# Narrow products kept together in a list schedule, attention bias strips read from DRAM, and a shorter inverse square root

## The chip, the cores and the metric

The kernel runs on one core of one Trainium2 chip. The metric is the device time of one execution in microseconds; lower is better. The whole program is one launch: two transformer-like blocks of two layers each, on 256 tokens of width 1024, batch one.

## The reference, cut to what matters

The first block has two layers of attention and feed-forward. Its attention adds a bias to the logits that depends on the distance of query and key alone (`rel_bias` looked up by `rel_bucket(q - k)`, for 12 heads), masks keys behind the query, and takes a softmax. Queries, keys and the attention's output are normalised by their root mean square. The second block mixes a short convolution, attention over latent and context tokens and a gated linear attention in each of two layers, modulated by vectors that come from `silu(c) @ w_ada`.

```python
logits = einsum(q, k) * scale + bias_tab[rel_bucket(qpos - kpos)]
logits = where(qpos >= kpos, logits, -inf); p = softmax(logits)
rms_norm(x, g) = x * rsqrt(mean(x * x) + 1e-6) * g
mod = silu(c) @ w_ada + b_ada        # and the same for c_ctx
```

Everything is in float32. The weights, about 270 MB, are read from DRAM once.

## The kernel before

**Tiling.** Activations lie transposed, 128 channels to a tile and 256 or 512 tokens along the free axis. Each weight arrives as a `raw` tile of 128 by 1024 (512 KB) by the sync queue (SP), is split into a rounded high part `wH` by ScalarE (ACT) and a remainder `wL` by VectorE (DVE), and each product is three passes of TensorE (PE): high by high, high by low, low by high (`mm3`). Layer 0 of the first block runs four head pairs one after another (`attention1`): two with `diff_pair`, two with `moba_pair`; then the output projection and the feed-forward (`ffn`).

**The order of the work.** The program records every operation (`record`) and then sets the order itself (`order`): a list schedule over five engines, with a cost for each operation, a latency, a priority (the place in the program) and limits on tiles. On each engine the operation of lowest priority number that is ready goes next. The engines then run their lists in that order, each waiting on semaphores where its data isn't there. Since every operation is issued from `emit` (L442), every row of the profile has that line, and groups are told apart by tiles. `nc.after` gives an operation one more predecessor in the schedule only; on the chip it makes no wait.

**Narrow products.** Column sums (`gsum`, tiles `xsq`, `qsq`, `osq`, `gsq`, `ksq` by a constant of 32 columns into a tile `ms`) and the modulation vectors (`mod_part`, tile `wada` by `cs`) are products whose stationary side has 32 columns. Four of them write the four quarters of the partitions of one PSUM tile. Each float32 product is two instructions, so a group of four is eight. The schedule's `cost` gives a whole product's time to the first of a group and 27 ns to each of the others.

**Bias strips.** `bias_strips` makes a row for every head (tile `brow`, 12 partitions by 384, in SBUF) of bias by distance, with the mask added. `bias_strip` spreads a head's row over 128 partitions, each shifted by one element, by a DMA of the ACT queue from the one partition that holds the row: 12 DMAs of 128 KB, two for each of 6 tiles `strip`. They are recorded once for each of layer 0's four pairs: one tile for each of the first two, two for each of the last two. `attn_scores` adds them to the scores on DVE (`sb<-x,s,strip`). Layer 1 uses the same strips again.

**Roots.** `rsqrt` works on small tiles (`s`, 1 to 16 columns) on DVE: a shift and a subtraction of the bits, and three Newton steps of three instructions; 12 instructions with the first addition, 13 with a scale. It is called 42 times, the last two in `out_last`, where the result is made.

Of the kernel before, what the change touches and what calls it, by code (L numbers as in the profile page):

```python
# [26 lines left out]
EPS = 1e-6  # L27
NEG = -1.0e30
MAGIC = 0x5F3759DF
AHEAD = {"ps": 12, "T": 16, "Q": 14}  # L30
ROLES = {"mm": 4, "x4": 4, "ms": 3, "raw": 4, "H": 7, "L": 7, "ada": 4}
NT, NQ = 24, 24
# [41 lines left out]

class Op:
    __slots__ = ("i", "eng", "fn", "args", "kw", "cost", "lat", "prio", "deps", "succ", "nd", "ready", "start", "end",
                 "new", "uses", "dma", "table", "alloc")


class _Proxy:  # L80
# [51 lines left out]
class Rec:  # L132


    def __init__(self, tc):
        self.tc, self.nc = tc, tc.nc
        nc = tc.nc
        self.vector, self.scalar, self.tensor = _Proxy(self, "DVE", nc.vector), _Proxy(self, "ACT", nc.scalar), _Proxy(self, "PE", nc.tensor)
        self.gpsimd, self.sync = _Proxy(self, "POOL", nc.gpsimd), _Proxy(self, "SP", nc.sync)
        self.ops, self.tiles, self.caps, self.psum, self.acc, self.role = [], {}, {}, set(), {}, {}  # L140
        self.seen, self.old = {}, set()
        self.offset = 0.0
        self.ahead, self.rolecap = {}, {}
        self.after = None

    def pool(self, ctx, name, bufs, **k):
        p = ctx.enter_context(self.tc.tile_pool(name=name, bufs=bufs, **k))
# [15 lines left out]
    def box(self, ap):  # L163
        pat = ap.ap
        ps, pn = pat[0]
        ps = ps or 1
        p0, f0 = divmod(ap.offset, ps) if pn > 1 or ps > 1 else (0, ap.offset)
        f1 = f0 + 1
        for s, c in pat[1:]:
            f1 += s * (c - 1)  # L170
        return p0, p0 + pn, f0, f1

    def cost(self, eng, method, out, args, kw):
# [38 lines left out]
    def record(self, eng, method, fn, args, kw):  # L212
        o = Op()
        o.i, o.eng, o.fn, o.args, o.kw = len(self.ops), eng, fn, args, kw
        o.prio = o.i + self.offset
        out = kw["out"] if "out" in kw else args[0]
        outs = [out] + ([kw["accum_out"]] if kw.get("accum_out") is not None else [])
        ins = [a for a in (args if "out" in kw else args[1:]) if isinstance(a, bass.AP)]
        ins += [a for k, a in kw.items() if isinstance(a, bass.AP) and k not in ("out", "accum_out")]
        o.lat = LAT[eng]  # L220
        o.table = TABLES.get(args[2]) if eng == "ACT" and method == "activation" else None
        o.dma = method == "dma_start"
        if method == "dma_start":
            o.lat = 0
        src_args = (out,) + tuple(args if "out" in kw else args[1:])
        o.cost = self.cost(eng, method, out, src_args, kw)
        deps, o.alloc = set(), set()
        o.uses = set()
        o.new = []
        if method == "dma_start":  # L230
            nb = self.free(out) * out.ap[0][1] * 4
            o.lat = nb
        for ap, w in [(a, False) for a in ins] + [(a, True) for a in outs]:
            tn = ap.tensor.name
            if tn not in self.tiles:
                continue
            if tn in self.old:
                pass
            elif tn not in self.seen:
                self.seen[tn] = o.i  # L240
                o.new.append(tn)
                o.uses.add(tn)
            else:
                o.uses.add(tn)
                o.alloc.add(self.seen[tn])
            b = self.box(ap)
            lst = self.acc.setdefault(tn, [])
            bank = tn in self.psum
            c = b
            if bank and eng == "PE" and w and (kw.get("start") or method == "transpose"):  # L250
                c = (b[0], b[1], 0, 1 << 30)
            keep = []
            for (pb, pi, pw, pe) in lst:
                if w or pw:
                    hit = pb[0] < c[1] and c[0] < pb[1] and pb[2] < c[3] and c[2] < pb[3]
                    if hit or (bank and pe != eng):
                        deps.add(pi)
                    if w and b[0] <= pb[0] and pb[1] <= b[1] and b[2] <= pb[2] and pb[3] <= b[3] and pi != o.i:
                        continue
                keep.append((pb, pi, pw, pe))  # L260
            keep.append((b, o.i, w, eng))
            self.acc[tn] = keep
        if self.after is not None:
            deps.add(self.after)
        deps.discard(o.i)
        o.alloc -= deps
        o.alloc.discard(o.i)
        o.deps = deps
        self.ops.append(o)

    def order(self):
# [73 lines left out]

        done = 0
        total = len(ops)
        while done < total:
            best = None
            for e in engs:  # L350
                t0 = t_eng[e]
                while future[e] and future[e][0][0] <= t0:
                    r, p, i = heapq.heappop(future[e])
                    heapq.heappush(avail[e], (p, i))
                if avail[e]:
                    s = t0
                elif future[e]:
# [5 lines left out]
            if best is None:  # L363
                raise RuntimeError("deadlock: " + str({k: [(ops[i].fn.__name__, ops[i].args[:1]) for i in v][:2] for k, v in parked.items() if v})[:2000])
            s, e = best
            t_eng[e] = max(t_eng[e], s)
            while future[e] and future[e][0][0] <= s:
                r, p, i = heapq.heappop(future[e])
                heapq.heappush(avail[e], (p, i))
            p, i = heapq.heappop(avail[e])  # L370
            o = ops[i]
            d = PATIENCE.get(e, 0)
            if d and o.cost > d:
# [41 lines left out]
            for j in o.succ:  # L415
# [7 lines left out]
                q.nd -= 1  # L423
                if q.nd == 0:
                    push(q)
            for tn in o.uses:
                left[tn] -= 1
                fin[tn] = max(fin.get(tn, 0.0), vis)
# [19 lines left out]
class Emit:  # L448
# [148 lines left out]

    def rsqrt(self, src, n, scale=None, shape=None, guard=None, more=None):
        nc = self.nc
        tiles = [self.small(n) for _ in range(5)] + [self.small(n, I32)]  # L600
        v, y, t, u, r, h = tiles
        sh = (lambda q: q) if shape is None else (lambda q: q.rearrange(shape[0], **shape[1]))
        bits = lambda q, dt: q.bitcast(dt)
        if more is not None:
            nc.vector.scalar_tensor_tensor(v, src, EPS, more, ALU.add, ALU.add)
        elif guard is None:
            nc.vector.tensor_scalar(sh(v), src, EPS, None, ALU.add)
        else:
            nc.vector.tensor_tensor(out=sh(v), in0=src, in1=guard, op=ALU.add)
        nc.vector.tensor_scalar(h, bits(tiles[0], I32), 1, None, ALU.logical_shift_right)  # L610
        nc.vector.tensor_scalar(bits(tiles[1], I32), h, -1, MAGIC, ALU.mult, ALU.add)
        for i in range(3):
            nc.vector.tensor_tensor(out=t, in0=y, in1=y, op=ALU.mult)
            nc.vector.scalar_tensor_tensor(u, t, -0.5, v, ALU.mult, ALU.mult)
            nc.vector.scalar_tensor_tensor(y, u, 1.5, y, ALU.add, ALU.mult)
        if scale is not None:
            nc.vector.tensor_scalar(r, y, scale, None, ALU.mult)
            return tiles[4]
        return tiles[1]

    def gsum(self, ps, sqs, ones, start=True, stop=True):

        nc = self.nc
        nc.after = max(nc.last(sq) for sq in sqs)
        for g, sq in enumerate(sqs):
            nc.tensor.matmul(ps[32 * g:32 * g + 32, :self.free(sq)], self.c(ones), sq, start=start, stop=stop)
        nc.after = None

    def gcols(self, ps, ng, n):

# [57 lines left out]
    def mod_part(self, l, part, after):  # L688
# [4 lines left out]
        for kk in range(0, KT, 2):  # L693
# [5 lines left out]
            if kk % 4:  # L699
                nc.after = nc.last(raw)  # L700
                for g in range(4):
                    nc.tensor.matmul(ps[32 * g:32 * g + 32, :], self.cs[:, kk - 2 + g, :], ws[g], start=kk < 4, stop=kk >= 4)
                nc.after = None
                ws = []
        res = self.t2("adar")
        nc.scalar.activation(res, ps, AF.Copy)
# [48 lines left out]
    def bias_strips(self):  # L755
# [7 lines left out]
        nc.tensor.matmul(ps[:12, :384], rb, oh, start=True, stop=True)  # L763
        nc.vector.tensor_tensor(out=row, in0=ps[:12, :384], in1=mr, op=ALU.add)
        self.strip = [None] * 6
        self.brow = row

    def bias_strip(self, i, after):

        nc = self.nc  # L770
        st = self.t2("strip")
        nc.after = after
        for a in range(2):
            src = self.brow[2 * i + a:2 * i + a + 1, 0:T]
            win = bass.AP(tensor=src.tensor, offset=src.offset + P - 1, ap=[list(src.ap[0]), [-1, P], [1, T]])
            nc.scalar.dma_start(st[:, a * T:(a + 1) * T], win)
        nc.after = None
        self.strip[i] = st.rearrange("p (a b) -> p a b", a=2)

    def lam(self, l, init):  # L780
        nc = self.nc
# [33 lines left out]
    def attn_scores(self, pr, a, qg, kn, rq, rcol, head):  # L815
# [10 lines left out]
        for m in range(2):  # L826
# [5 lines left out]
            for t in range(2):  # L832
                nk = P * (t + 1)
                sl = slice(t * P, t * P + nk)
                nc.vector.scalar_tensor_tensor(sb[:, sl], ps[:, t * T:t * T + nk], rq[:, rcol(m, t):rcol(m, t) + 1],
                                               st[:, T - nk:T], ALU.mult, ALU.add)
                nc.vector.tensor_reduce(mx[:, t:t + 1], sb[:, sl], AX.X, ALU.max, negate=True)
                nc.scalar.activation(sb[:, sl], sb[:, sl], AF.Exp, bias=mx[:, t:t + 1], accum_out=den[:, t:t + 1])
            rc = self.small(2)
# [977 lines left out]
def constants():  # L1817
# [30 lines left out]
    for lv in range(7):  # L1848
# [1 line left out]
        seg = i // (2 * m)  # L1850
        half = (i // m) % 2
        masks[:, lv, :] = (seg[:, None] == seg[None, :]) & (half[:, None] != half[None, :])
    return {"ck": ck, "oneh": oneh.astype(np.float32), "maskr": np.ascontiguousarray(maskr.astype(np.float32)),
            "masks": masks.reshape(P, 7 * P).astype(np.float32)}


# [23 lines left out]
```

## Time and profile before

| | |
|---|---|
| three timed runs | median 2057.44 us (2056.23 to 2058.48) |
| profiled execution | 2054.4 us, its span 2052.6 us |
| PE busy | 2027.0 us (99%), 14158 instructions |
| DVE busy | 1464.4 us (71%) |
| ACT busy | 1167.6 us (57%) |
| read from DRAM | 282.51 MB, 140 GB/s over the span |

Busy time counts instructions of the engine itself; time in which an engine's sequencer waits or issues a DMA isn't counted. In the views, a row of a timeline gives the start in us, the length in us, the engine (with a q behind it: the engine's sequencer), the operation with its output and inputs, shapes and count, and in brackets the idle time ahead of it with what ended it. Neighbouring instructions of one kind are merged into one row.

### The profile page before, as it was taken

The numbers are of one execution on the slowest core, as the hardware profiler recorded it, in microseconds if no ns is written. First come the engines' busy times: TensorE is split into PE (matmuls) and PEld (weight loads), VectorE is DVE, ScalarE is ACT, GpSimd is POOL, SyncE is SP. The second block draws the span as 40 slices with busy tenths as digits, with TensorE's granted clock in tenths as the row PEclk, the third lists the DMA queues.
The fourth block names the chain that finished last, engine by engine and source line by source line (L and its number), as shares of the span: only waits on it lengthen the run. The fifth ranks groups of instructions, "written<-read, shape, count | busy, mean of one in ns | idle before, by whom it ended". The sixth has DMA issues, their size and how long they took to land.

```text
span 2052.6 us, 35592 instructions
## 1 busy us (share of the span) xinstructions
PE 2027.0 (99%) x14158; PEld 1847.7 (90%) x14158; DVE 1464.4 (71%) x2846; ACT 1167.6 (57%) x2055; POOL 8.7 (0%) x20
## 2 busy tenths in 40 slices
PE   9989999999999999999999999999999999999998
PEld 7879999989999989988888888888888999999997
DVE  7778986888866699983477755563467888696663
ACT  6656656767665767762366323333357777575542
POOL 0000000000000000000000000000000000000000
PEclk9999999999999999999999999999999999999999
DMA  9765665555555121232122543342361225436551
GB/s 296 140 166 200 225 226 174 185 175 175 206 185 196 60 74 64 72 120 86 53 72 72 193 135 122 115 140 96 135 214 67 89 83 186 141 116 215 176 190 68
DMA packets 86846, 292.68 MB, mean 143 GB/s; under 512 B 9452, under 2 KB 17176, under 8 KB 86424
## 3 DMA queue, kind: packets, MB, share of 16 engines
q1 hardware_dynamic: 81544, 281.50, 39.6%
q10 hardware_dynamic: 5136, 8.91, 2.8%
q8 instruction: 111, 1.82, 0.4%
q14 instruction: 55, 0.45, 0.1%
HBM read 282.51 MB, written 4.19 MB: 140 GB/s over the span
## 4 chain that ended last, share of the span: by engine, by line
PE 97%; DMA 1%; DVE 1%; ACT 0%; issue 0%; ACTq 0%; SPq 0%; DVEq 0%
PE mm L442 78%; PE x L442 11%; PE acc L442 6%; PE ms L442 2%; DMA strip<-brow 1%; DVE s L442 0%; DMA xx<-in_xt_dram 0%; ACTq L442 0%; ACT h L442 0%; DVE wL L442 0%; DVE sb L442 0%; ACT y L442 0%; ACT wH L442 0%; ACT xg L442 0%; DVE h L442 0%
## 5 line engine op out<-in xcount | busy, mean ns | idle before, releaser
L442 DVE TENSOR_TENSOR wL<-raw,wH 128x1024 fp32r<-128x1024 f32 (+1 forms) x472 | 569.7, 1217 | 307.0 <-PE mm L442 144.6
L442 ACT ACTIVATE wH<-raw 128x1024 fp32r<-128x1024 f32 (+1 forms) x472 | 491.5, 1053 | 252.2 <-DVE wL L442 112.0
L442 PE MATMUL mm<-h2H,wH 128*128 128x256 f32 (+1 forms) x1504 | 504.2, 338 | 2.1 <-ACT h2H L442 2.1
L442 PE MATMUL mm<-h2L,wH 128*128 128x512 f32 (+2 forms) x1504 | 504.0, 337 | 0.0
L442 PE MATMUL mm<-h2H,wL 128*128 128x256 f32 (+1 forms) x1472 | 497.5, 338 | 0.0
L442 PEld LDWEIGHTS mm<-h2H,wH 128*128 128x128 f32 x1504 | 283.6, 190 | 33.2 <-issue 3.5
L442 PEld LDWEIGHTS mm<-h2L,wH 128*128 128x128 f32 (+1 forms) x1504 | 283.2, 189 | 28.7 <-issue 1.6
L442 PEld LDWEIGHTS mm<-h2H,wL 128*128 128x128 f32 x1472 | 279.3, 190 | 28.6 <-issue 1.0
L442 PE MATMUL mm<-h,wH 128*128 128x256 f32 x1216 | 219.6, 283 | 0.0
L442 PEld LDWEIGHTS mm<-h,wH 128*128 128x128 f32 x1216 | 189.6, 192 | 0.0
L442 PE MATMUL mm<-h,wL 128*128 128x256 f32 x608 | 172.0, 283 | 0.0
L442 PE MATMUL mm<-xg,wH 128*128 128x256 f32 x704 | 133.9, 289 | 1.5 <-ACT wH L442 1.5
L442 PE MATMUL acc<-hid,wH 128*128 128x256 f32 x704 | 128.2, 284 | 0.0
L442 PEld LDWEIGHTS mm<-h,wL 128*128 128x128 f32 x608 | 116.7, 192 | 0.0
L442 PEld LDWEIGHTS mm<-xg,wH 128*128 128x128 f32 x704 | 112.1, 195 | 4.0 <-ACT wH L442 1.9
L442 PE MATMUL mm<-xL,wH 128*128 128x512 f32 (+1 forms) x320 | 111.4, 348 | 0.0
L442 PE MATMUL mm<-xH,wL 128*128 128x512 f32 (+1 forms) x320 | 111.2, 348 | 0.0
L442 PE MATMUL mm<-xH,wH 128*128 128x512 f32 (+1 forms) x320 | 111.0, 348 | 0.0
L442 PEld LDWEIGHTS acc<-hid,wH 128*128 128x128 f32 x704 | 109.8, 192 | 0.8 <-issue 0.8
L442 PE MATMUL mm<-xg,wL 128*128 128x256 f32 x352 | 101.6, 290 | 0.2 <-DVE wL L442 0.2
L442 PE MATMUL acc<-hid,wL 128*128 128x256 f32 x352 | 98.4, 283 | 0.0
L442 ACT ACTIVATE gt<-mm,hb 128x512 f32<-128x512 f32 (+1 forms) x48 | 27.8, 579 | 116.1 <-PE mm L442 116.0
(295 smaller groups left out, 3850.5 us busy)
## 6 DMA issues: line engine op xcount, KB each, us to landing
raw<-in_w_dram SPq DMA_DIRECT2D x272, 512.0 KB, 3.7
raw<-in_w1up_dram SPq DMA_DIRECT2D x88, 512.0 KB, 4.1
wada<-in_wada_dram SPq DMA_DIRECT2D x48, 512.0 KB, 5.4
raw<-in_w1in_dram SPq DMA_DIRECT2D x46, 512.0 KB, 5.9
raw<-in_w1dn_dram SPq DMA_DIRECT2D x44, 512.0 KB, 4.4
raw<-in_w1out_dram SPq DMA_DIRECT2D x16, 512.0 KB, 4.5
crow<-in_crow_dram SPq DMA_DIRECT2D x6, 512.0 KB, 6.4
qh<-qh SPq DMA_DIRECT2D x16, 128.0 KB, 2.2
```

Of the source, the lines that this page charges most:

```text
L442: o.fn(*o.args, **o.kw)
```

## The change

It has three parts. Operations recorded while `join` is set are scheduled directly behind the operation recorded before them, if they are ready then; `gsum` and `mod_part` set it for the second to fourth product of a group. `brow` is now a tile in DRAM: the sync queue stores the rows there, and loads each `strip` (both heads, 256 KB) by one DMA, with 128 overlapping windows. The rows are stored in reverse and the strip is read with a step of -1 by DVE. `rsqrt` becomes nine instructions, with the scale folded in, and takes five small tiles.

```diff
@@ def order(self):
+        must = None
+        gone = set()
 ...
+            if must is not None:
+                e, i = ops[must].eng, must
+                p, s = ops[i].prio, max(t_eng[e], ops[i].ready)
+                gone.add(i)
+                must = None
+            else:
 ...
+            if o.i + 1 < total and ops[o.i + 1].join and ops[o.i + 1].nd == 0:
+                must = o.i + 1
@@ def rsqrt(self, src, n, scale=None, shape=None, guard=None, more=None):
-        nc.vector.tensor_scalar(h, bits(tiles[0], I32), 1, None, ALU.logical_shift_right)
-        nc.vector.tensor_scalar(bits(tiles[1], I32), h, -1, MAGIC, ALU.mult, ALU.add)
-        for i in range(3):
-            nc.vector.tensor_tensor(out=t, in0=y, in1=y, op=ALU.mult)
-            nc.vector.scalar_tensor_tensor(u, t, -0.5, v, ALU.mult, ALU.mult)
-            nc.vector.scalar_tensor_tensor(y, u, 1.5, y, ALU.add, ALU.mult)
-        if scale is not None:
-            nc.vector.tensor_scalar(r, y, scale, None, ALU.mult)
+        f = RQ[0] * (1.0 if scale is None else scale)
+        nc.vector.tensor_scalar(y.bitcast(I32), v.bitcast(I32), -0.5, MAGIC, ALU.mult, ALU.add)
+        nc.vector.tensor_tensor(out=t, in0=y, in1=y, op=ALU.mult)
+        nc.vector.tensor_tensor(out=w, in0=t, in1=v, op=ALU.mult)
+        nc.vector.scalar_tensor_tensor(w, w, RQ[1], w, ALU.add, ALU.mult)
+        nc.vector.scalar_tensor_tensor(y, w, RQ[2], y, ALU.add, ALU.mult)
+        nc.vector.tensor_tensor(out=t, in0=y, in1=y, op=ALU.mult)
+        nc.vector.scalar_tensor_tensor(w, t, -0.5 * f * RQ[0] ** 2, v, ALU.mult, ALU.mult)
+        nc.vector.scalar_tensor_tensor(r, w, 1.5 * f, y, ALU.add, ALU.mult)
@@ def gsum(self, ps, sqs, ones, start=True, stop=True):
         for g, sq in enumerate(sqs):
+            nc.join = g > 0
             nc.tensor.matmul(ps[32 * g:32 * g + 32, :self.free(sq)], self.c(ones), sq, start=start, stop=stop)
@@ def mod_part(self, l, part, after):
                 for g in range(4):
+                    nc.join = g > 0
@@ def bias_strips(self):
-        self.brow = row
+        self.brow = nc.dram_tile(self.tc, [12, 384], "brow")
+        nc.sync.dma_start(self.brow, row)
+        self.bstore = len(nc.ops) - 1
@@ def bias_strip(self, i, after):
-        nc.after = after
-        for a in range(2):
-            src = self.brow[2 * i + a:2 * i + a + 1, 0:T]
-            win = bass.AP(tensor=src.tensor, offset=src.offset + P - 1, ap=[list(src.ap[0]), [-1, P], [1, T]])
-            nc.scalar.dma_start(st[:, a * T:(a + 1) * T], win)
+        src = self.brow[2 * i:2 * i + 1, 0:T]
+        win = bass.AP(tensor=src.tensor, offset=src.offset + 1, ap=[[1, P], [384, 2], [1, T]])
+        nc.after = max(after, self.bstore)
+        nc.sync.dma_start(st, win)
@@ def attn_scores(self, pr, a, qg, kn, rq, rcol, head):
+                e = st[:, nk - 1:nk]
+                bias = bass.AP(tensor=e.tensor, offset=e.offset, ap=[list(e.ap[0]), [-1, nk]])
                 nc.vector.scalar_tensor_tensor(sb[:, sl], ps[:, t * T:t * T + nk], rq[:, rcol(m, t):rcol(m, t) + 1],
-                                               st[:, T - nk:T], ALU.mult, ALU.add)
+                                               bias, ALU.mult, ALU.add)
```

The left-out lines record `join` with each operation, skip entries in the schedule's lists that were taken out of turn, let the address boxes count negative steps, and reverse the constants `oneh` and `maskr` on the host.

## Rows read from the trace of the kernel before

**Rows 1.** The page's first part: busy time of each engine.

```profile
PE 2027.0 (99%) x14158; PEld 1847.7 (90%) x14158; DVE 1464.4 (71%) x2846; ACT 1167.6 (57%) x2055; POOL 8.7 (0%) x20
```

**Rows 2.** Windows: stretch, length, busy us (count) per engine, clock, DMA share, GB/s.

```profile
8.20:60.00 51.80, 51.80 (x405) 44.96 (x406) 39.97 (x111) 38.30 (x78) 2.08 (x4) 0.97 0.97 293
60.00:91.70 31.70, 31.70 (x259) 27.99 (x257) 23.16 (x78) 18.88 (x45) 1.04 (x2) 1.00 0.70 155
91.70:138.00 46.30, 36.11 (x253) 31.02 (x252) 34.76 (x89) 27.63 (x67) 0.00 (x0) 0.96 0.75 137
...
347.80:490.20 142.40, 140.53 (x1141) 126.04 (x1141) 113.52 (x311) 98.78 (x209) 3.29 (x6) 1.00 0.53 178
```

**Rows 3.** The chain that ended last, in order of time: start, us, what.

```profile
91.78 3.79 issue
...
116.33 18.58 DMA strip<-brow
```

**Rows 4.** Timeline of ACT and its queue, layer 0 of the first block.

```profile
80.29 0.53 ACTq L442 DMA_DIRECT2D strip<-brow  x1
...
84.29 5.18 ACTq L442 DMA_DIRECT2D strip<-brow  x1
89.56 2.01 ACT L442 ACTIVATE wH<-raw 128x1024 fp32r<-128x1024 f32 x2 [6.86 <-issue]
...
113.19 8.31 ACTq L442 DMA_DIRECT2D strip<-brow  x3
```

**Rows 5.** Timeline of DVE around the bias rows and the strips' uses.

```profile
30.76 0.54 DVE L442 TENSOR_TENSOR brow<-ms,maskr 12x384 f32<-12x384 f32 x1
...
39.14 0.74 DVE L442 SCALAR_TENSOR_TENSOR sb<-x,s,strip 128x128 f32<-128x128 f32 x2 [1.14 <-DMA strip<-brow]
...
97.37 0.74 DVE L442 SCALAR_TENSOR_TENSOR sb<-x,s,strip 128x128 f32<-128x128 f32 x2
```

**Rows 6.** DMA from 80 to 100 us: queue, packets, MB, share of 16 engines.

```profile
q10 hardware_dynamic: 522, 0.48, 60.4%
```

**Rows 7.** DMA issues of the whole run: count, KB each, median us to landing.

```profile
wd<-in_wd_dram SPq DMA_DIRECT2D x8, 128.0 KB, 4.1
...
crow<-in_crow_dram SPq DMA_DIRECT2D x6, 512.0 KB, 6.4
```

**Rows 8.** Tile raw from 0 to 170 us: the weights' landing times.

```profile
DMA to landing us min/median/max: 3.1/6.5/15.1
```

**Rows 9.** Timeline of PE at narrow products, broken groups and a whole one.

```profile
44.69 1.90 PE L442 MATMUL x<-wada,cs 128*32 128x512 f32 x10
...
70.14 1.04 PE L442 MATMUL x<-wada,cs 128*32 128x512 f32 x2
71.12 0.55 PE L442 MATMUL x<-ck,sb 128*128 128x128 f32 x3
71.59 1.06 PE L442 MATMUL x<-wada,cs 128*32 128x512 f32 x8
...
109.78 0.62 PE L442 MATMUL ms<-qsq,ck 128*32 128x256 f32 x2
110.33 0.86 PE L442 MATMUL x<-at,v 128*64 128x256 f32 x4
...
152.63 0.64 PE L442 MATMUL ms<-xsq,ck 128*32 128x256 f32 x8
```

**Rows 10.** Timeline of DVE in the last root, and its use.

```profile
2045.80 0.15 DVE L442 SCALAR_TENSOR_TENSOR s<-s 128x1 f32<-128x1 f32 x1
...
2048.10 1.42 DVE L442 SCALAR_TENSOR_TENSOR y<-og,s,xt 128x512 f32<-128x512 f32 x2
```

**Rows 11.** Timeline of PE in layer 1: a wait for a root.

```profile
393.56 0.65 PE L442 MATMUL ms<-ck,s 128*128 128x128 f32 x4 [1.27 <-DVE s L442]
```

**Rows 12.** Timeline of the sync queue in layer 0.

```profile
57.45 8.85 SPq L442 DMA_DIRECT2D raw<-in_w1in_dram  x3
75.35 1.18 SPq L442 DMA_DIRECT2D qh<-qh  x2
```

More of the change, by code (lines that the diff above doesn't have):

```diff
@@ L29 @@
 MAGIC = 0x5F3759DF
+RQ = (0.3755374238926038, -3.334362783627379, 4.997213710402795)
 AHEAD = {"ps": 12, "T": 16, "Q": 14}
@@ L76 @@
     __slots__ = ("i", "eng", "fn", "args", "kw", "cost", "lat", "prio", "deps", "succ", "nd", "ready", "start", "end",
-                 "new", "uses", "dma", "table", "alloc")
+                 "new", "uses", "dma", "table", "alloc", "join")
 class _Proxy:
@@ L144, in __init__ @@
         self.after = None
+        self.join = False
     def pool(self, ctx, name, bufs, **k):
@@ L169, in box @@
         for s, c in pat[1:]:
-            f1 += s * (c - 1)
+            if s < 0:
+                f0 += s * (c - 1)
+            else:
+                f1 += s * (c - 1)
         return p0, p0 + pn, f0, f1
@@ L215, in record @@
         o.prio = o.i + self.offset
+        o.join = self.join
         out = kw["out"] if "out" in kw else args[0]
@@ L351, in order @@
                 t0 = t_eng[e]
-                while future[e] and future[e][0][0] <= t0:
+                while future[e] and (future[e][0][0] <= t0 or future[e][0][2] in gone):
                     r, p, i = heapq.heappop(future[e])
                     heapq.heappush(avail[e], (p, i))
+                while avail[e] and avail[e][0][1] in gone:
+                    heapq.heappop(avail[e])
                 if avail[e]:
@@ L365, in order @@
             s, e = best
[L366 to L370, printed above, removed]
+            if must is not None:
[3 more added lines that the diff above has]
+                must = None
+            else:
+                t_eng[e] = max(t_eng[e], s)
+                while future[e] and future[e][0][0] <= s:
+                    r, p, i = heapq.heappop(future[e])
+                    if i not in gone:
+                        heapq.heappush(avail[e], (p, i))
+                p, i = heapq.heappop(avail[e])
             o = ops[i]
@@ L599, in rsqrt @@
         nc = self.nc
-        tiles = [self.small(n) for _ in range(5)] + [self.small(n, I32)]
-        v, y, t, u, r, h = tiles
+        v, y, t, w, r = tiles = [self.small(n) for _ in range(5)]
         sh = (lambda q: q) if shape is None else (lambda q: q.rearrange(shape[0], **shape[1]))
-        bits = lambda q, dt: q.bitcast(dt)
         if more is not None:
@@ L609, in rsqrt @@
             nc.vector.tensor_tensor(out=sh(v), in0=src, in1=guard, op=ALU.add)
-        nc.vector.tensor_scalar(h, bits(tiles[0], I32), 1, None, ALU.logical_shift_right)
-        nc.vector.tensor_scalar(bits(tiles[1], I32), h, -1, MAGIC, ALU.mult, ALU.add)
-        for i in range(3):
-            nc.vector.tensor_tensor(out=t, in0=y, in1=y, op=ALU.mult)
-            nc.vector.scalar_tensor_tensor(u, t, -0.5, v, ALU.mult, ALU.mult)
-            nc.vector.scalar_tensor_tensor(y, u, 1.5, y, ALU.add, ALU.mult)
-        if scale is not None:
-            nc.vector.tensor_scalar(r, y, scale, None, ALU.mult)
-            return tiles[4]
-        return tiles[1]
+        f = RQ[0] * (1.0 if scale is None else scale)
[7 more added lines that the diff above has]
+        nc.vector.scalar_tensor_tensor(r, w, 1.5 * f, y, ALU.add, ALU.mult)
+        return r
     def gsum(self, ps, sqs, ones, start=True, stop=True):
@@ L625, in gsum @@
         for g, sq in enumerate(sqs):
+            nc.join = g > 0
             nc.tensor.matmul(ps[32 * g:32 * g + 32, :self.free(sq)], self.c(ones), sq, start=start, stop=stop)
-        nc.after = None
+        nc.after, nc.join = None, False
     def gcols(self, ps, ng, n):
@@ L701, in mod_part @@
                 for g in range(4):
+                    nc.join = g > 0
                     nc.tensor.matmul(ps[32 * g:32 * g + 32, :], self.cs[:, kk - 2 + g, :], ws[g], start=kk < 4, stop=kk >= 4)
-                nc.after = None
+                nc.after, nc.join = None, False
                 ws = []
@@ L765, in bias_strips @@
         self.strip = [None] * 6
-        self.brow = row
+        self.brow = nc.dram_tile(self.tc, [12, 384], "brow")
+        nc.sync.dma_start(self.brow, row)
+        self.bstore = len(nc.ops) - 1
     def bias_strip(self, i, after):
         nc = self.nc
-        st = self.t2("strip")
-        nc.after = after
-        for a in range(2):
-            src = self.brow[2 * i + a:2 * i + a + 1, 0:T]
-            win = bass.AP(tensor=src.tensor, offset=src.offset + P - 1, ap=[list(src.ap[0]), [-1, P], [1, T]])
-            nc.scalar.dma_start(st[:, a * T:(a + 1) * T], win)
+        st = self.t2("strip").rearrange("p (a b) -> p a b", a=2)
+        src = self.brow[2 * i:2 * i + 1, 0:T]
+        win = bass.AP(tensor=src.tensor, offset=src.offset + 1, ap=[[1, P], [384, 2], [1, T]])
+        nc.after = max(after, self.bstore)
+        nc.sync.dma_start(st, win)
         nc.after = None
-        self.strip[i] = st.rearrange("p (a b) -> p a b", a=2)
+        self.strip[i] = st
     def lam(self, l, init):
@@ L1852, in constants @@
         masks[:, lv, :] = (seg[:, None] == seg[None, :]) & (half[:, None] != half[None, :])
-    return {"ck": ck, "oneh": oneh.astype(np.float32), "maskr": np.ascontiguousarray(maskr.astype(np.float32)),
+    return {"ck": ck, "oneh": np.ascontiguousarray(oneh[:, ::-1].astype(np.float32)), "maskr": np.ascontiguousarray(maskr[:, ::-1].astype(np.float32)),
             "masks": masks.reshape(P, 7 * P).astype(np.float32)}
```

## The prediction

> **What bounds the kernel now.** I read the busy times first: PE is busy for 2027.0 us of a span of 2052.6, while DVE has 71% and ACT 57% [rows 1]. So the end is PE's work plus PE's pauses, and a change can win only by taking work off PE, by closing a pause, or by shortening what follows PE's last product. Then I asked where the 25.6 us of pauses lie, by windows. From 8.2 to 91.7 us PE has none; from 91.7 to 138 us it is busy 36.11 of 46.30 us, so 10.19 us are lost in the attention of layer 0; the attention and output projection of layer 1, the same work with the strips already there, lose 142.40 - 140.53 = 1.87 us [rows 2]. The rest is the start, the tail behind the last product, and waits of under 2 us. The third view was the chain of waits: in the stretch that loses 10 us it goes through "issue" for 3.79 us at 91.78 and through one strip's DMA for 18.58 us at 116.33 [rows 3]. The timeline of ACT says what that is. Issuing one strip took ACT's queue 5.18 us, and three more 8.31 us; behind the first ones ACT sat idle 6.86 us before it could split the next weight [rows 4]. PE's pause at 91.78 follows from that. The second cause is the transfer itself: from 80 to 100 us the queue that carries the strips moved 0.48 MB and held the 16 DMA engines 60.4% of the time [rows 6], so 0.604 x 20 = 12.1 us of all engines for 0.48 MB, or 40 GB/s, where the stretch before 60 us moves 293 GB/s [rows 2].
>
> **The strips.** Removed: 12 DMAs on ACT's queue. Added: one store of 18 KB and six loads of 256 KB on the sync queue. The store and a load can't be seen in this trace. The nearest row is `wd`, 256 pieces of 512 bytes from DRAM to 128 partitions, landing after 4.1 us; `crow`, 512 KB read by all partitions from the same 4 KB of DRAM, takes 6.4 us among other traffic [rows 7]. A strip has 256 pieces of 1 KB from one small region; I take 5 us from issue to landing, with 4.1 below, and above the 18.58 us that the slowest strip takes now. Strips 2 and 3 are issued at 80.29 and first used at 97.37 [rows 4, 5]; 17 us hold even a doubled landing time. So I count the strip pauses as gone except what layer 1 also has: 10.19 - 1.87 = 8.3 us. ACT is relieved of the issue time, and DVE, PE and the weights of their waits for it, in the same stretch.
>
> Strip 0 gets a detour. Its rows are ready at 31.3 and its first use, at 39.14, already waits 1.14 us for it [rows 5]. The store goes behind the weights; at their median landing time of 6.5 us [rows 8] it lands at about 37.8, and the load behind it at 41.9 to 44.2. The first scores are then 3 to 5 us later. In this stretch PE has no pause [rows 2] and other products to run, and weights no longer queue behind two slow strips; I charge 1.0 us, between 0 and 5. The issues themselves, seven on the sync queue, cost nothing there: that queue issued nothing between 66.3 and 75.35 [rows 12] while PE was fully busy.
>
> [...]
>
> **Groups kept together.** A group of four is eight instructions and takes 0.64 us at 256 columns, a piece of two 0.62 [rows 9]: the four run beside each other, so a piece costs what the whole does. A broken group costs another 0.55 us (109.78 to the next product at 110.33). I counted four such groups, at 48.65, 109.78, 385.51 and 411.06: 2.2 us. For the modulation (512 columns) a whole group takes 1.06 us and a lone product 0.98 (70.14 to 71.12) [rows 9]; two are broken so, at 70.14 and 1543.65: 1.9 us. Three more, at 44.69, 408.97 and 438.22, show as ten instructions in 1.90 us, a group with the first product of the next behind it: 1.90 - 1.06 = 0.84 each, 2.5 us. Two groups at 79.3 lie interleaved, and about 0.1 us is lost when they are parted. Sum: 6.5 us. All lie where PE is the limit, or will be once the strips are gone, so I count all of it. Should the forced order not reach the chip, it is 0.
>
> **Roots.** The last root is on the path behind PE's last product: 12 instructions from 2045.80 to 2048.10, 0.19 us each [rows 10]. Three fewer give 0.6 us. Of the others, 42 calls in all, the one that shows as a wait of PE for a root, 1.27 us in layer 1 [rows 11], gets shorter by the same 0.6. The rest, 42 x 3 x 0.19 = some 24 us of DVE, is hidden by PE's work.
>
> **The reversed read** of the strip on DVE isn't in this trace. The 64 additions have the same elements and bytes; I take 0. If it were at half speed, each of 0.37 us (0.74 for two [rows 5]) would cost up to 0.4 more, 13 us of DVE in each layer, where DVE is free 142.40 - 113.52 = 29 us [rows 2]; a quarter to a half on the chain is 3 to 6 us a layer at worst. I see no gain in it.
>
> **Sum.** 8.3 + 6.5 + 0.6 + 0.6 - 1.0 = 15.0 us. The profiled execution took 2054.4, its span 2052.6; that makes 2039.4. The median of the timed runs is 3.0 above the profiled one, so I forecast 2057.44 - 15.0 = 2042.4.
>
> **Rivals.**
>
> *The strips were a symptom.* If the attention of layer 0 is held by its chain of small steps, the 10.19 us come back as other waits, and 2057.44 - 6.5 - 1.2 + 1.0 = 2050.7 remains. For it: all engines are busy 70 to 80% there. Against it: layer 1 does the same with 1.87 us. 10%.
>
> *Groups aren't kept together on the chip*, or their pieces ran in time that PE had to spare: 2042.4 + 6.5 = 2048.9. For it: 4 of the 9 broken groups lie ahead of or between the strips' pauses, which could have absorbed them. Against: the pauses begin with ACT's release, which the forecast moves. 10%.
>
> *The reversed read is slow* or the whole order, which is redone from the new costs, is less lucky: 2 to 8 us lost, 2044 to 2050, as 2047. Waits of 1 to 2 us are now at three places, and a new order may have more. 15%.
>
> *The sync queue is blocked: slower.* Its list is in order. A strip's load waits for a free tile, and the first for the store; all weights stand behind it, then ACT and DVE that split them, then PE. It was silent for 9 us at 66.3 and PE had no pause [rows 2, 12], so 9 us are covered. With landings of 15.1 us as the longest weights have [rows 8], each of four pairs would lose 15.1 - 9 = 6.1 us, 24 us in all: 2066. It decides against the change from 9 + 15.0/4 = 12.8 us of blocking at each pair. The long landings are themselves the strips' doing, which speaks against it. 5%.
>
> **How the numbers follow.** The forecast's own case has 60%, with 2038 to 2046 from the bounds of the detour (0 to 5 us), of what layer 1 keeps (0 to 1.87) and of the waits on roots. Taking in the rivals at 2047, 2048.9 and 2050.7 up to the edge, the range is 2036 to 2051. What a measurement of this kernel can tell from no change is 0.2%, or 4.1 us: faster is below 2053.3. All cases but the blocked queue and the tails of two others lie there: faster 0.89, same 0.06, slower 0.05.
>
> **What would show it.** Right: PE's busy time falls by about 6.5 us, to 2020; every `wada`, `qsq` and `xsq` row of PE has eight instructions or a multiple; no strip on ACT's queue, and no idle of ACT for "issue" near 89; strips land in 4 to 7 us; PE's pause between 91 and 138 falls from 10.2 to about 2 us; the last root takes 1.7 us instead of 2.3. Wrong: strips that land in over 15 us, waits of DVE for strips, gaps on PE near 40 us, additions of strips over 0.5 us, or new pauses behind the first 200 us.

## The result, and the profile after

The changed kernel takes 2034.7 us (median of 4 runs, 2033.21 to 2035.8) beside 2056.84 us for the kernel before; the ratio is 0.9891 (95% interval 0.9874 to 0.9908). The forecast was 2042.4 with a range from 2036.0. The direction was right, the gain of 22.1 us half as large again as the 15.0 us forecast, and the time 1.3 us below the range.

Its profiled execution took 2035.6 us (span 2033.8), against 2054.4 (2052.6) before: 18.8 us less. The first line of its page answers to [rows 1]: PE's busy time fell by 7.6 us, DVE's by 19.9.

```profile
PE 2019.4 (99%) x14158; PEld 1846.6 (91%) x14158; DVE 1444.5 (71%) x2712; ACT 1168.7 (57%) x2055; POOL 8.6 (0%) x20
```

Windows of the changed kernel, as in [rows 2] (stretch, length, busy us of PE, PEld, DVE, ACT, POOL, granted clock, DMA share, GB/s; the last stretch is layer 1, which now lies earlier):

```profile
8.20:60.00 51.80, 49.61 (x392) 43.41 (x394) 41.03 (x101) 40.00 (x81) 2.07 (x4) 0.97 0.90 328
60.00:91.70 31.70, 31.08 (x251) 28.28 (x252) 26.77 (x78) 21.95 (x52) 1.04 (x2) 0.95 0.45 148
91.70:138.00 46.30, 45.83 (x356) 41.48 (x355) 35.61 (x89) 30.08 (x69) 0.00 (x0) 1.00 0.39 131
...
337.50:478.00 140.50, 140.50 (x1165) 129.06 (x1162) 114.03 (x297) 101.57 (x215) 3.17 (x6) 1.00 0.53 182
```

PE now loses 0.47 us between 91.7 and 138 where it lost 10.19, and nothing in layer 1 where it lost 1.87. New are some 2.5 us of short pauses between 55 and 61 us, and a granted clock of 0.95 in the stretch from 60 on. The strips' own rows show why the long pauses are gone (instructions of the tile: min/median/max ns, first and last start; then the landing times):

```profile
L462 DVE SCALAR_TENSOR_TENSOR sb<-x,s,strip x64: 324/405/478, 47.1 to 442.5; 128x128 f32<-128x128 f32 x32, 128x256 f32<-128x256 f32 x32
L462 SPq DMA_DIRECT2D strip<-brow x6: 380/426/932, 36.3 to 105.1; - x6
...
DMA to landing us min/median/max: 5.2/5.6/7.4
```

Strips land after 5.6 us, not 11.6, no instruction waits for one, and the reversed read costs nothing: its 64 additions took 327/406/477 ns before. On PE every row of `wada`, `qsq` and `xsq` now has eight instructions, or sixteen where two groups stand side by side (timeline, as in [rows 9]). One `osq` group still runs in two pieces, at 58.65 and 59.96 us, because its second half isn't ready: it waits 0.90 us for ACT.

```profile
47.27 0.64 PE L462 MATMUL ms<-qsq,ck 128*32 128x256 f32 x8
47.72 1.90 PE L462 MATMUL x<-wada,cs 128*32 128x512 f32 x16
...
396.07 1.92 PE L462 MATMUL x<-wada,cs 128*32 128x512 f32 x16
```

PE's rows for the modulation products fell from 17.3 to 12.3 us and those for `qsq` from 12.0 to 9.4, 7.6 us together. The last root takes 1.73 us (2027.75 to 2029.48) instead of 2.30 [rows 10]:

```profile
2027.75 0.15 DVE L462 SCALAR_TENSOR_TENSOR s<-s 128x1 f32<-128x1 f32 x1
...
2029.48 1.41 DVE L462 SCALAR_TENSOR_TENSOR y<-og,s,xt 128x512 f32<-128x512 f32 x2
```

By the profile, then: 10.4 us of pauses of PE, 7.6 us of its busy time, 0.8 us of the tail. In the forecast these were 7.3 + 0.6, 6.5 and 0.6. The other 3.3 us lie between profile and timed runs: the kernel before is 2.4 us slower in its timed runs than in its profiled execution (3.0 by the three runs that the forecast had), the changed one 0.9 us faster.

### The profile page after: what moved, and what is told of

Read it like the earlier page. It is cut to its first block, busy times and chain, and to the rows that moved or that the text cites. A ratio compares the mean times of both kernels' runs of the same rounds, so it can differ in the third digit from the quotient of the medians.

```text
span 2033.8 us, 35473 instructions
## 1 busy us (share of the span) xinstructions
PE 2019.4 (99%) x14158; PEld 1846.6 (91%) x14158; DVE 1444.5 (71%) x2712; ACT 1168.7 (57%) x2055; POOL 8.6 (0%) x20
## 4 chain that ended last, share of the span: by engine, by line
PE 98%; DMA 1%; ACT 1%; DVE 0%; issue 0%; SPq 0%; DVEq 0%; ACTq 0%
PE mm L462 79%; PE x L462 11%; PE acc L462 6%; PE ms L462 2%; DMA raw<-in_w_dram 0%; DMA raw<-in_w1in_dram 0%; ACT wH L462 0%; ACT fH L462 0%; DVE s L462 0%; ACT F L462 0%; SPq L462 0%; ACT att L462 0%; ACT h L462 0%; ACT v L462 0%; DVE y L462 0%
```

## The experiments

The parts were run alone, each part was taken out of the whole, one part was varied, and one cost was measured by itself. Times are medians; the ratio is to the kernel before on the same chip. The clock is the mean granted clock of the profiled execution; busy time, and pauses up to the last product, are PE's, from the same one.

| run | time us | ratio (95%) | clock | PE busy | pauses |
|---|---|---|---|---|---|
| before (in the first set) | 2057.39 | | 0.998 | 2027.0 | 17.4 |
| e1 groups alone | 2053.11 | 0.9980 (0.9971 to 0.9989) | 0.995 | 2021.2 | 21.3 |
| e2 strips alone | 2044.51 | 0.9940 (0.9927 to 0.9954) | 0.999 | 2024.4 | 10.3 |
| e3 roots alone | 2055.35 | 0.9992 (0.9983 to 1.0001) | 0.997 | 2027.9 | 17.6 |
| e4 all | 2033.87 | 0.9884 (0.9871 to 0.9898) | 0.998 | 2016.8 | 7.9 |
| e5 all but groups | 2041.62 | 0.9919 (0.9905 to 0.9932) | 0.999 | 2023.9 | 7.1 |
| e6 all but roots | 2040.24 | 0.9913 (0.9900 to 0.9927) | 0.998 | 2019.9 | 10.1 |
| e7 strips, ACT's queue | 2045.55 | 0.9935 (0.9921 to 0.9948) | 0.998 | 2025.2 | 11.1 |
| e8 all, and pairs | 2026.10 | 0.9844 (0.9831 to 0.9858) | 0.999 | 2009.5 | 7.1 |
| e9 all but strips | 2052.82 | 0.9972 (0.9961 to 0.9984) | 0.993 | 2023.9 | 19.2 |
| e10 all, 4 short holds | 2038.23 | 0.9901 (0.9886 to 0.9916) | 0.998 | 2019.0 | 10.2 |
| e11 all, 4 long holds | 2063.99 | 1.0028 (1.0019 to 1.0038) | 0.995 | 2026.3 | 28.0 |

The kernel before was at 2058.42 in the set of e5 to e8 and at 2058.48 in that of e9 to e11, so differences across sets carry about 1 us.

**e1, groups alone.** The edit is the change's `join` and nothing else:

```diff
 ...
+            if o.i + 1 < total and ops[o.i + 1].join and ops[o.i + 1].nd == 0:
+                must = o.i + 1
 ...
+            nc.join = g > 0
 ...
```

> The kernel before with the groups of four kept together and nothing else. Theory A (the parts add up, each by its own mechanism): PE's busy time falls by the 6.5 us that I forecast, or by the 7.6 us that the changed kernel shows (2027.0 to 2019.4), no narrow row with two, six or ten instructions is left, and the time falls by as much, 6 to 8 us. Rival B (four of the nine broken groups lie ahead of or between the strips' pauses, which absorb what they give back): PE's busy time falls as much, but its pauses grow by about 2.8 us, and the time falls by 3 to 5 us.

The time fell by 4.3 us: B's size. The busy time fell by 5.8 us, and the pauses rose by 3.9, a little more than B's 2.8. Windows of e1 show the two pauses of the strips, and the clock right behind each:

```profile
87.40:90.90 3.50, 0.16 (x2) 0.07 (x1) 1.99 (x4) 3.45 (x8) 0.00 (x0) 0.97 0.79 31
90.90:94.30 3.40, 3.40 (x17) 3.40 (x18) 3.34 (x7) 2.17 (x3) 0.00 (x0) 0.53 0.80 26
...
111.50:119.40 7.90, 0.16 (x2) 0.05 (x1) 0.00 (x0) 1.43 (x3) 0.00 (x0) 0.69 0.90 124
119.40:125.00 5.60, 5.60 (x27) 5.60 (x28) 4.54 (x15) 1.79 (x2) 0.00 (x0) 0.52 0.93 132
```

PE did nothing for 3.3 and 7.7 us, and then worked for 3.4 and 5.6 us at a granted clock of 0.53 and 0.52; a product `mm<-wL,xg` of 256 columns took 0.41 us behind the second pause (at 120.27) and 0.28 ahead of it (at 111.34). That clock isn't a pause in any view: the windows count it as busy PE (3.40 of 3.40 and 5.60 of 5.60 us).

**e2, strips alone.** The change's store, loads and reversed read; groups and roots as before.

```diff
 ...
+        nc.sync.dma_start(self.brow, row)
 ...
-            nc.scalar.dma_start(st[:, a * T:(a + 1) * T], win)
 ...
+        nc.sync.dma_start(st, win)
 ...
```

> The kernel before with the strips stored to DRAM and loaded by the sync queue, and with the reversed read; groups and roots as before. Theory A: PE's pauses between 20 and 140 us fall from 10.2 to about 3 us, strips land in 5 to 7.5 us, and the time falls by 7 to 8 us. Rival C (the strips were a symptom; the shorter roots or the groups closed the pauses): the pauses stay at 6 us or more and the time falls by under 4 us.

The pauses did what theory A says, 17.4 to 10.3 in all, and no view shows the clock low between 20 and 138 us:

```profile
20.00:60.00 40.00, 39.08 (x309) 32.46 (x307) 33.40 (x96) 28.13 (x57) 1.04 (x2) 1.00 0.85 298
60.00:91.70 31.70, 30.86 (x248) 27.09 (x249) 27.04 (x87) 22.09 (x51) 1.04 (x2) 1.00 0.47 153
91.70:138.00 46.30, 45.67 (x347) 40.57 (x346) 36.07 (x93) 29.73 (x68) 0.00 (x0) 1.00 0.39 132
```

But the time fell by 12.9 us, not 7 to 8. The clock is what A left out. In the kernel before, PE worked at a granted clock of 0.64 for 4.3 us behind the strip's pause:

```profile
91.70:95.70 4.00, 0.21 (x2) 0.16 (x2) 3.37 (x6) 3.95 (x8) 0.00 (x0) 1.00 0.88 79
95.70:100.00 4.30, 4.30 (x25) 4.23 (x26) 4.27 (x12) 2.84 (x9) 0.00 (x0) 0.64 0.86 98
```

The profiles show 10.0 of the 12.9 us: 7.1 of pauses, 2.6 of busy time, and the tail. By an estimate from its clock, (1 - 0.64) x 4.3 = 1.5 of the 2.6 us stand in the second line. Not all of the rest is the strips': in the first 20 us the kernel before has a granted clock of 0.91 and 0.92, e2 of 1.00, and the changed kernel, without the strips' pauses, falls there too (0.83 from 10 to 20 us). The last 2.9 us stand in no profile: the timed runs of the kernel before, at a mean clock of 0.993 to 0.998, lie 3.0 us above its profiled one, and e2's, at 0.997 to 0.999, 0.1.

**e3, roots alone.**

```diff
 ...
-        for i in range(3):
 ...
+        nc.vector.tensor_scalar(y.bitcast(I32), v.bitcast(I32), -0.5, MAGIC, ALU.mult, ALU.add)
 ...
```

> The kernel before with the nine-instruction root alone. My forecast gave this part 1.2 us (0.6 in the tail, 0.6 in one wait). Theory A': it closes the waits of layer 1 (1.87 us) and the one before the second block's second layer (1.94 us) nearly whole, and the time falls by 3 to 4 us. Rival D: those waits went by the new order or by the other parts; here the time falls by 0.5 to 1.3 us.

The time fell by 2.0 us, between the two, and the interval of the ratio just reaches 1. The pauses of layer 1 are gone and that before the second block's second layer fell to 0.2 us, but in this order the strips' first pause was 7.3 us instead of 3.8.

**e4, the change again**, without an edit.

> The changed kernel once more on the same chip as the three parts. Theory A: its gain is the sum of the three parts within 2 us. Rival E (the order that the whole gives is lucky by itself): the sum of the parts falls short by 4 us or more. By the profile the gain is 18.8 us, by the timed runs 22.1; should the timed kernel before be 2 to 3 us above its own profiled execution here too, the difference lies in the runs of before and not in a part of the change.

The sum of the parts, 4.3 + 12.9 + 2.0 = 19.2 us, falls short of the whole, 23.5, by 4.3 us. That is E's size, but e5, e6 and e9, each with an order of its own, give a plainer reading than luck: a part pays less while another's pauses stand.

**e5, all but the groups; e6, all but the roots.** The edits take e1's and e3's lines out of the changed kernel.

> The changed kernel without the groups kept together (strips and roots as changed). The groups alone gave 4.1 us, with PE's pauses up from 17.4 to 21.3 us and two more stretches at the lower clock. Theory A2 (what the groups give back was swallowed by the strips' pauses and by the clock that falls after them): here, where those pauses are gone, the groups are worth their whole 6.5 to 7.6 us, and the time is 2040 to 2042 us. Rival B2 (a broken group costs only what was measured alone): 2037 to 2038 us.

> The changed kernel with the old root of 12 or 13 instructions. Theory A2: the shorter root closes the pauses of layer 1 (1.87 us) and before the second block's second layer (1.94 us) and 0.6 us of the tail, so without it the time is 3 to 4 us more, 2037 to 2038 us. Rival D2: as measured alone, 1 to 2 us more, 2035 to 2036 us.

With the strips' pauses gone, the groups are worth 7.7 us (6.7 with the 1.0 us between the sets taken out), and the roots 6.4 (5.3). A2 holds for the groups, and both theories were too low for the roots. e6 shows why; windows around the pause of 1.95 us before the second block's second layer:

```profile
1533.10:1535.20 2.10, 0.15 (x2) 0.09 (x1) 2.00 (x7) 1.87 (x5) 0.00 (x0) 1.00 0.00 0
1535.20:1540.00 4.80, 4.80 (x28) 4.80 (x29) 3.04 (x10) 4.80 (x13) 0.00 (x0) 0.64 0.01 3
```

and the same place in the changed kernel:

```profile
1532.00:1535.00 3.00, 2.71 (x21) 2.37 (x20) 2.84 (x9) 3.00 (x9) 0.00 (x0) 1.00 0.02 5
1535.00:1543.00 8.00, 8.00 (x70) 8.00 (x69) 4.84 (x9) 7.21 (x16) 0.00 (x0) 1.00 0.06 17
```

The old root leaves a pause of 1.95 us, and behind it the clock was 0.64 for 4.8 us: (1 - 0.64) x 4.8 = 1.7 us of PE's work, an estimate. With the new root 0.29 us of pause are left, and the clock stayed at 1.00. This isn't a matter of one order: all five profiled kernels with the old root wait 1.94 or 1.95 us there and 1.26 or 1.27 us for a root in layer 1, and none with the new root waits over 0.3 us at either place. The pauses (2.2 us), the tail (0.6) and this fall of the clock (1.7) make 4.5 of the 5.8 us between the profiled executions of e6 and e4; the rest is not explained. Such a pause isn't followed by the lower clock in every execution: the kernel before had the same 1.94 us pause, and its profile shows the clock at 1.00 behind it:

```profile
1549.20:1551.30 2.10, 0.16 (x2) 0.09 (x1) 2.00 (x7) 2.02 (x5) 0.00 (x0) 1.00 0.00 0
1551.30:1562.00 10.70, 10.70 (x90) 10.70 (x91) 7.53 (x17) 9.77 (x22) 0.00 (x0) 1.00 0.05 14
```

**e7, the strips' source against their queue.** e2 with one line back on ACT's queue:

```diff
-        nc.sync.dma_start(st, win)
+        nc.scalar.dma_start(st, win)
```

> The kernel before with strips from DRAM, but loaded by ACT's queue as before (one load for a tile, groups and roots as before). Theory S (the source decides: one partition's bytes are slow to read, which holds the DMA engines and makes the issuing queue stand): loads are issued in under 1 us each, land in 4 to 8 us, PE's pauses between 20 and 140 us are 2 to 4 us, the granted clock is 0.998 or 0.999, and the time is 2044 to 2046 us, as with the sync queue. Rival Q (ACT stands because it issues them): issues of 2 us and more and idle ACT remain, and the time is 2049 us or more.

S holds in its time (2045.55 us), its clock (0.998) and its issues (0.39 us, median). The queue makes no difference to the time that can be measured (ratios 0.9935 and 0.9940, the intervals overlap), though the loads landed after 3.8 us here and after 5.2 in e2 (medians); rows of the tile, then its landing times:

```profile
L445 ACTq DMA_DIRECT2D strip<-brow x6: 366/392/487, 40.8 to 112.9; - x6
...
DMA to landing us min/median/max: 3.3/3.8/5.6
```

ACT's issues took up to 5.2 us each before and under 0.5 us here, so it isn't ACT's issuing that makes them long. That the source in one partition makes them long is the author's estimate, from [rows 6]; e7 doesn't isolate it: with the source, the loads became one of 256 KB for two of 128 KB, and the direction of their windows turned. The sync queue with the old source wasn't tried.

**e9, all but the strips.** The changed kernel with `bias_strips`, `bias_strip`, the read in `attn_scores` and the constants as before.

> The changed kernel with the strips as before (from one partition, by ACT's queue); groups and roots as changed. Theory K (the strips cost their pauses and the stretches at the lower clock behind them): PE's pauses between 80 and 145 us are again 10 us or more, the granted clock is 0.994 to 0.996, and the time is 2047 to 2050 us, so that the strips are worth 13 to 16 us in the whole. Rival: pauses alone, 7 to 8 us in the whole, 2041 to 2042 us.

K holds and its size was too low: the strips are worth 18.9 us in the whole (17.9 with the sets' difference taken out), and the time is 2.8 us above K's range. Taken out one at a time, the parts come to 6.7 + 5.3 + 17.9 = 29.9 us, more than the whole has: each hides a part of the others' losses, so these figures can't be added. Windows of e9:

```profile
89.10:96.70 7.60, 0.25 (x3) 0.10 (x1) 2.70 (x5) 4.11 (x7) 0.00 (x0) 0.83 0.78 26
96.70:101.00 4.30, 4.30 (x20) 4.30 (x21) 4.21 (x11) 2.12 (x8) 0.00 (x0) 0.50 0.80 26
...
122.00:140.00 18.00, 11.16 (x48) 8.92 (x46) 10.15 (x29) 10.79 (x26) 0.00 (x0) 0.67 0.87 159
```

**e10 and e11, what a pause costs by itself.** The changed kernel, with PE held four times in a stretch where it has no pause, by a product that reads what GpSimd clears once or six times:

```diff
+            if l == 0 and b == 1 and j % 2:
+                z = self.t4("hold").rearrange("p a b -> p (a b)")
+                nc.scalar.activation(z[:, :1], th[:, :1], AF.Copy)
+                for _ in range(6):  # 1 in e10
+                    nc.gpsimd.memset(z, 0.0)
+                    nc.ops[-1].cost = 1
+                nc.tensor.matmul(self.ps_m()[:, :P], z[:, :P], z[:, :P], start=True, stop=True)
```

> The changed kernel with four short holds of PE, 30 us apart, in a stretch of the second block where PE has no pause: at every second step of one gate, PE gets a product that reads a tile which GpSimd has just cleared once (about 1 us, which the schedule believes to be next to nothing). The product's result is used by nothing. Both theories: four pauses of 0.5 to 1.2 us, no stretch at the lower clock near them, and the time is up by the pauses' sum, 2 to 5 us.

> The same with six clears in a row before each of the four products (about 6 us). Theory K (a pause of 2 us and more costs more than its length, since the granted clock then falls to half for a stretch): four pauses of 4 to 6 us, each followed by a stretch at half the clock of 3.4 us or more, PE's busy time up by 1.7 us or more for each, and the time up by the pauses' sum and 7 us or more. Rival L (a pause costs its length): the time is up by the pauses' sum, 16 to 24 us, with PE's busy time as in the changed kernel.

PE's waits for these tiles (us in total, times, longest), in e10 and in e11:

```profile
PE ms L462 <- POOL hold L462: 1.8, 4, 0.5
```

```profile
PE ms L462 <- POOL hold L462: 19.2, 4, 4.8
```

e10 costs 4.4 us beside e4. Its pauses are shorter than expected, 1.8 us in all, and PE's busy time is up by 2.2, which is no more than the 2.6 by which two executions of one kernel differ (the changed kernel and e4, 2019.4 and 2016.8). The clock was 1.00 over the stretch with all four holds:

```profile
1120.00:1220.00 100.00, 98.19 (x433) 80.14 (x432) 62.88 (x83) 31.59 (x38) 3.82 (x4) 1.00 0.48 158
```

e11 costs 30.1 us beside e4: 19.2 of pauses, and busy time up by 9.5. Taking e10's 2.2 off leaves 7.3 us, 1.8 for each pause, for the clock. It is rather 2.1: e10 and e11, of one set, differ by 25.8 us in time and by 17.4 in these waits, and the other 8.4 us are 2.1 for each. (The profiled busy times say less because the clock fell at the start of e10, to 0.92 and 0.91 in its first two stretches of 10 us, and not in e11, with 1.00 and 1.00.) Windows of e11 at the first pause:

```profile
1120.00:1134.60 14.60, 14.60 (x65) 11.75 (x63) 12.20 (x17) 7.95 (x10) 1.33 (x2) 1.00 0.79 284
1134.60:1139.30 4.70, 0.02 (x1) 0.02 (x1) 4.61 (x8) 0.00 (x0) 4.40 (x5) 0.85 0.41 122
1139.30:1144.00 4.70, 4.70 (x12) 3.83 (x13) 2.43 (x5) 1.06 (x1) 0.00 (x0) 0.50 0.45 139
1144.00:1163.00 19.00, 19.00 (x83) 15.67 (x83) 7.40 (x11) 3.96 (x6) 0.31 (x1) 0.98 0.38 131
```

K holds for these four pauses: 1.00 before the first, 0.50 for 4.7 us behind it, and 0.98 in the 19 us after that; behind the other three the clock is 0.53 for 3.5 us, 0.52 for 5.5 and 0.61 for 4.0. That it holds for every pause from 2 us on isn't shown: the kernel before had 1.00 behind its 1.94 us.

**e8, a version beyond the change.** `moba_pair`'s two heads write the two halves of one PSUM tile with products of 64 columns. The edit takes them in turn and keeps them together:

```diff
 ...
+                ats.append(self.attn_transpose(s))
+            nc.after = max(nc.last(at) for at in ats)
+            for t in range(2):
+                for m in range(2):
 ...
+                    nc.join = t + m > 0
+                    nc.tensor.matmul(o[:, t * P:T], v[:, t, vc], ats[m][:, t * T:T + t * P], start=t == 0, stop=t == 1)
 ...
```

> The changed kernel, and in moba_pair the two heads' products of 64 columns (at by v, upper and lower half of one PSUM tile) side by side, head by head in turn and kept together. In the changed kernel 16 such products of four instructions take 0.79 us each, all apart; in the kernel before one pair stood together by chance and its eight instructions took 0.81 us. Theory A: 8 x 0.8 = 6.4 us less, 2027 to 2029 us. Rival P (the first head now waits for the second's softmax and transposes, and PE has too little other work there): pauses of 0.5 to 1 us at each pair, and the time is 2031 to 2034 us.

```profile
97.51 0.87 PE L462 MATMUL x<-at,v 128*64 128x256 f32 x8
```

Eight instructions now take the 0.87 us that four took in [rows 9] (0.86 at 110.33). PE's busy time fell by 7.3 us, its pauses by 0.8, and the time to 2026.1 us, 1.6% under the kernel before. Some 1.7 of the 7.3 us, an estimate, are the lower clock in e4's first 20 us (0.93 and 0.90; 1.00 here). The gain over e4, 7.8 us across the two sets, is a little more than the 6.4 us of A, and the time 0.9 us below A's range; P is refuted.

## Why the prediction was wrong

- **The strips' pauses**, 7.3 us with the detour: right. e2 lost 7.1 us of pauses. It has 1.8 us of new ones between 20 and 91.7 us, nearly all near 56 and 60, where 1.0 was charged for the detour. The first scores came 8.0 us later in the changed kernel (47.10 for 39.14), not 3 to 5. Every kernel with strips from DRAM pauses there and none with the old strips does (from 52 to 63 us PE is busy 8.53 of 11.00 us in the changed kernel and 11.00 in the one before); that the late scores are the cause is likely, not shown.
- **The strips' price**: this is the step that failed. It priced a pause of PE at its length, and had no term for the clock. e11 shows that a pause of 4.8 us costs 6.6 to 6.9, because PE then worked for 3.5 to 5.5 us at a granted clock of 0.50 to 0.61. The strips alone gave 12.9 us. [rows 2] had the sign: the granted clock was 0.96 in the stretch of the pauses. All four rivals lay on the slow side; none asked what would make the gain larger.
- **"The median of the timed runs is 3.0 above the profiled one"**, carried over as a constant: wrong for the same reason. In 45 timed executions of the kernel before the mean granted clock was 0.993 to 0.998, most often 0.994; those at 0.993 and 0.994 have medians of 2059.0 and 2058.5 us, the only one at 0.998 took 2054.9. The profiled execution, with 0.998, was among the best; it showed one fall of the clock behind the strips' pauses, e1 and e9 show more. The changed kernel's timed runs have 0.998 and 0.999. The 3.0 us were mostly the strips' too, to judge by e2, whose timed runs lie only 0.1 us above its profile. Where in the 45 executions the clock fell isn't shown.
- **The groups**, 6.5 us: about right in the whole (6.7 to 7.7), but not alone (4.3); the second rival, that the strips' pauses absorb a part, described e1.
- **The roots**, 1.2 us: the term was mis-sized, 5.3 to 6.4 in the whole. The tail's 0.6 was right. I counted one wait of PE and left out the pause of 1.94 us before the second block's second layer, which shows as a wait for ACT, some steps behind the root, and the fall of the clock behind it (0.64 for 4.8 us in e6, none in the kernel before).
- **The reversed read** at 0, **the sync queue** that loses nothing, **the landing** at 5 us (5.6): right. The slower rival didn't occur.
- In sum: the gain was 7.1 us above the forecast. 3.3 of them lie between profile and timed runs, where the constant was carried over, 2.5 are pauses (more closed in layer 0 and by the roots, less 1.5 at the detour), 1.1 busy time and 0.2 the tail.
- What stays open: in which executions a pause of some 2 us is followed by the lower clock, and in which not; and why the clock falls in the first 20 us of some executions.

## What to carry to other kernels

Price a pause of TensorE at its length and, where the clock falls behind it, at what that takes away: by an estimate (1 - 0.50) x 4.7 = 2.4 us behind e11's first pause, 1.8 to 2.1 for each of its four by the times. So look at the granted clock right behind each pause: busy time hides it (e1: 3.40 of 3.40 us busy at 0.53). A part of a change that gives back work is worth less while another pause takes it (the groups 4.3 us alone, 6.7 to 7.7 in the whole), so begin with the pauses. Narrow products that write different partitions of one PSUM tile belong next to each other in the list: a lone one took 0.98 us and a whole group 1.06 [rows 9].

## What the runs showed of the hardware that was not expected

- Four pauses of 4.7 to 4.85 us cost 1.8 to 2.1 us each beyond their length (e11); four of 0.3 to 0.5 us showed no such cost (e10).
- Spreading 128 KB out of one partition of SBUF landed after 7.1 to 18.6 us and held the issuing queue up to 5.2 us (the kernel before); 256 KB as overlapping windows of 1 KB from DRAM landed after 3.3 to 7.4 us with issues under 1 us (e7 and the changed kernel).
- The first 8207 products of PE are in the same order in e10 and e11, and yet the clock in the first 20 us was 0.92 and 0.91 in one and 1.00 in the other: some 1.7 us, an estimate from these clocks, between two profiled executions that no change made.
- Two products of 64 columns to the two halves of one PSUM tile, taken in turn, took 0.87 us (eight instructions, e8); one alone took 0.86 (four, [rows 9]).
